# Attention scores in three 64-row products, two heads at a time, in place of two 128-row products, one head at a time

## The chip, the cores and the metric

The kernel runs on one core of a Trainium2 chip. The metric is the device time of one execution in microseconds. Before the change it was 1157.51 us, the median of 3 runs (1156.15 to 1157.67). The engines that matter are TensorE (matmul; its weight loads are shown apart), VectorE, ScalarE and GpSimd; in the profile's names PE and PEld, DVE, ACT and POOL. SyncE issues the DMAs.

## The reference

Two layers of a trunk with two token mixers side by side. There are 512 latent tokens and 256 context tokens of 1024 channels; all heads have 64 channels.

```python
def _attend(q, k, v):
    s = jnp.einsum('bqkgd,btkd->bkgqt', q, k).astype(jnp.float32) * (HEAD_DIM ** -0.5)
    p = jax.nn.softmax(s, axis=-1).astype(v.dtype)
    return jnp.einsum('bkgqt,btkd->bqkgd', p, v)
...
    a_att = _na_latent(qa, ka, va, cka, cva, rpb, rows)     # 8 heads, 8x16 window + all context keys
    b_att = _gqa_latent(qb, k_all, v_all)                   # 8 query heads on 2 key heads, all 768 keys
    out_x = _merge(a_att, b_att, a_z, b_z, g_a, g_b, w_o_a, w_o_b, w_out)
    x_new = x + gate_x * out_x
    if update_ctx:                                          # layer 0 only
        c_a_att = _attend(cqa, cka, cva).reshape(B, L, NA_WIDTH)
        c_b_att = _attend(cqb, ckb, cvb).reshape(B, L, GQA_WIDTH)
```

`_na_latent` is the neighbourhood attention: a latent query sees a window of latent keys with a learned bias, and all 256 context keys without one. `_gqa_latent` is the grouped attention. In layer 0 the context tokens attend to the context keys too, in both.

## The kernel before

Everything that is multiplied is kept as two parts of the fast 32-bit matmul type: `hi`, the rounded value, and `lo`, the rest. A product is then `hi*hi + hi*lo + lo*hi`, three matmuls (`mm3`, L339 to L343). Projections run over 128 channels at a time; activations lie with channels on partitions, so a matmul has a 128x128 stationary part (whose load is the PEld row) and up to 512 columns that stream.

A head has only 64 channels. Two heads lie in one group of 128 partitions, the even head in the lower 64 and the odd head in the upper 64. The scores of a head use all 128 rows of the array in this way: `stage_q` (L694, casts at L699, L700) makes a tile `qs` with q's hi part in the head's own half and q's lo part in the other half. `stage_k` (L685) makes `kh`, which has k's hi part in both halves (L688, L689), and `kl`, which has k's lo part in the own half (L690) and zeros, or in the grouped attention the same lo part (L692), in the other. Two matmuls then make the scores (`scores`, L703, and L783 for the tiles with two runs of keys): `qs` against `kh` gives hi*hi + lo*hi, `qs` against `kl` gives hi*lo.

The neighbourhood attention (`na_first`, `na_scores`) handles a head as 4 tiles of 128 queries with 512 keys each, of which 256 are window and 256 context. The bias is added, and the row's maximum found, in one VectorE operation from PSUM (L786), then comes exp (L789) and the normalization (`softmax_tail`, L639; its multiplication on VectorE at L644, or on GpSimd at L647). The grouped attention (`gq_first`, `gq_scores`) has 4 tiles of 128 queries with 768 keys, so 1.5 PSUM banks each: the maximum at L943, exp from PSUM at L945. In layer 0 every head also has one context tile (`ctx_scores`): two blocks of 128 queries by 256 keys.

`na_values` and `gq_values` then transpose the probabilities on the array (L655, L657), split them in hi and lo (`transpose_split`, ScalarE at L660, VectorE at L661) and multiply them with the values (L809 to L820, L960, L961). `head_out` (L664) multiplies the result into the gate.

`pipeline` (L825) sets the order for a whole attention: the scores of head h, then the values of head h-1, then a share of `fill`, which is a list of projection matmuls that need nothing of the attention. The text of the program gives priorities; a planner places each instruction on its engine's queue from a model of time, so an instruction with a later place in the text can go ahead of one that has to wait. `behind` (L376) ties instructions of one engine to the order in which they were written. `bg` is a list of background steps on VectorE, dot products of the modulation weights (`ada_steps`, L220, each tile of weights loaded by a DMA).

The PSUM has 8 banks. Of these the neighbourhood attention gives scores three tiles of one bank (`s`) and values one (`v`), and the grouped attention gives scores two tiles of two banks and values one. A tile of probabilities, `p`, comes from a pool with `NP_NA` and `NP_GQ` buffers for layers 0 and 1.

## Time and profile before

| what | value |
|---|---|
| median of 3 runs | 1157.51 us |
| the profiled execution | 1154.84 us, span 1153.1 us |
| granted TensorE clock | 0.998 |
| PE busy | 1123.5 us (97%) |
| DVE busy | 811.9 us (70%) |
| ACT busy | 573.2 us (50%) |
| POOL busy | 494.5 us (43%) |

The span is the time from the first to the last instruction of the profiled execution; a little of its time lies around the span. By the start times of the matmuls of the scores (L706, L707, L783) the neighbourhood attention of layer 0 lies at about 152 to 320 us of the span, the grouped attention of layer 0 at 386 to 600, the neighbourhood attention of layer 1 at 780 to 893, and the grouped attention of layer 1 at 948 to 1086. A row of the timeline gives the start, the duration, the engine, the line, the operation with its output and inputs, and the shape; the duration of a matmul runs from its start to the modelled end of its pass through the array, so that matmuls that follow each other overlap in the rows. What a matmul takes from the array's time is the distance between the starts.

### The profile page before, as it was taken

To read this page: it belongs to the slowest core of one execution; us is meant where nothing else is said; L and a number is where in the kernel's file an instruction comes from. 1 tells how busy PE (TensorE), PEld (TensorE's weight loads), DVE (VectorE), ACT (ScalarE), POOL (GpSimd) and SP (SyncE) were. 2 spreads that over 40 slices of the span, in tenths; PEclk is the share of its full clock that TensorE was granted. 3 is DMA by queue.
4 is the path that set the end of the run, shared out by engine and by line. 5 is a ranking of instruction groups with operands and counts; after the bars stand their busy time and mean duration, and the time that the engine had idled before them with its cause. 6 is when DMAs were issued, how large, how long until landed. Compare 5 with 4: busy or idle time off the path is not lost.

```text
span 1153.1 us, 17284 instructions
## 1 busy us (share of the span) xinstructions
PE 1123.5 (97%) x6078; PEld 949.3 (82%) x6078; DVE 811.9 (70%) x1508; ACT 573.2 (50%) x1167; POOL 494.5 (43%) x459
## 2 busy tenths in 40 slices
PE   5999999999999999999999999999999999999998
PEld 4688888889988888878788887888888988887786
DVE  4566688897474687688587755569787765898563
ACT  5453266666433465566330265446666445766521
POOL 3372354454266243354411126245553664365311
PEclk9999999999999999999999999999999999999999
DMA  9544222233342332470353523543332333142133
GB/s 370 194 125 137 69 85 65 73 115 96 115 130 60 109 102 73 65 279 19 114 179 101 174 74 110 173 108 114 107 105 84 110 101 101 65 173 92 62 130 93
DMA packets 87999, 134.04 MB, mean 116 GB/s; under 512 B 10628, under 2 KB 52584, under 8 KB 86248
## 3 DMA queue, kind: packets, MB, share of 16 engines
q1 hardware_dynamic: 87912, 132.94, 36.7%
q8 instruction: 48, 0.79, 0.3%
q14 instruction: 39, 0.32, 0.1%
HBM read 115.58 MB, written 17.32 MB: 115 GB/s over the span
## 4 chain that ended last, share of the span: by engine, by line
PE 83%; DVE 7%; issue 3%; POOL 2%; ACT 2%; DMA 1%; ACTq 0%; POOLq 0%; DVEq 0%
PE psx L341 12%; PE psx L343 12%; PE psx L342 12%; PE psf L341 9%; PE psf L342 9%; PE psf L343 9%; PE pst L657 4%; PE pss L706 2%; PE pss L707 2%; PE psv L961 2%; PE pss L783 1%; PE psv L960 1%; PE pst L417 1%; DVE wlo L328 1%; DVE ptl L661 1%
## 5 line engine op out<-in xcount | busy, mean ns | idle before, releaser
L661 DVE TENSOR_TENSOR ptl<-pst,pth 128x512 fp32r<-128x512 f32 (+1 forms) x176 | 116.0, 672 | 46.4 <-ACT pth L660 45.4
L660 ACT CAST pth<-pst 128x512 fp32r<-128x512 f32 (+1 forms) x176 | 99.2, 576 | 87.6 <-PE pst L657 56.3
L328 POOL TENSOR_TENSOR wlo<-raw,whi 128x512 fp32r<-128x512 f32 x68 | 95.5, 1408 | 107.2 <-ACT whi L326 86.2
L341 PE MATMUL psf<-hx,whi 128*128 128x512 f32 (+1 forms) x368 | 139.2, 378 | 0.0
L342 PE MATMUL psf<-hx,whi 128*128 128x512 f32 (+1 forms) x368 | 138.1, 375 | 0.0
L343 PE MATMUL psf<-hx,wlo 128*128 128x512 f32 (+1 forms) x368 | 137.8, 374 | 0.0
L341 PE MATMUL psx<-whi,hx 128*128 128x512 f32 (+1 forms) x368 | 137.6, 375 | 0.0
L342 PE MATMUL psx<-wlo,hx 128*128 128x512 f32 (+1 forms) x368 | 135.8, 369 | 0.0
L343 PE MATMUL psx<-whi,hx 128*128 128x512 f32 (+1 forms) x368 | 133.4, 369 | 0.0
L314 POOL TENSOR_TENSOR wlo<-raw,whi 128x512 fp32r<-128x512 f32 x44 | 61.4, 1397 | 140.4 <-ACT whi L311 123.8
L326 ACT CAST whi<-raw 128x512 fp32r<-128x512 f32 x136 | 82.4, 621 | 55.6 <-DMA raw<-in_w_in_dram 39.6
L311 ACT CAST whi<-raw 128x512 fp32r<-128x512 f32 x96 | 58.7, 623 | 102.1 <-PE psx L343 38.6
L657 PE MATMUL pst<-ident,p 128*128 128x128 f32 x640 | 99.9, 272 | 1.4 <-DVE ptl L661 0.9
L328 DVE TENSOR_TENSOR wlo<-raw,whi 128x512 fp32r<-128x512 f32 x68 | 72.1, 1062 | 28.4 <-ACT whi L326 27.8
L657 PEld LDWEIGHTS pst<-ident,p 128*128 128x128 f32 x640 | 77.8, 140 | 13.3 <-DVE ptl L661 1.6
L646 POOL TENSOR_SCALAR r<-r 128x1 f32<-128x1 f32 x64 | 23.1, 361 | 151.8 <-DVE r L641 144.2
L647 POOL TENSOR_TENSOR p<-p,r 128x512 f32<-128x512 f32 (+1 forms) x64 | 83.4, 1304 | 5.0
L341 PEld LDWEIGHTS psx<-whi,hx 128*128 128x128 f32 x368 | 69.7, 189 | 11.7 <-issue 0.8
L343 PEld LDWEIGHTS psx<-whi,hx 128*128 128x128 f32 x368 | 69.4, 189 | 11.8
L343 PEld LDWEIGHTS psf<-hx,wlo 128*128 128x128 f32 x368 | 69.4, 188 | 11.8
L342 PEld LDWEIGHTS psx<-wlo,hx 128*128 128x128 f32 x368 | 69.7, 189 | 10.8
L341 PEld LDWEIGHTS psf<-hx,whi 128*128 128x128 f32 x368 | 69.4, 189 | 10.8 <-ACT zt L502 0.2
(239 smaller groups left out, 3032.6 us busy)
## 6 DMA issues: line engine op xcount, KB each, us to landing
raw<-in_w_in_dram SPq DMA_DIRECT2D x168, 256.0 KB, 2.9
rawb<-in_w_ada_dram SPq DMA_DIRECT2D x64, 256.0 KB, 2.8
gs<-zt SPq DMA_DIRECT2D x32, 256.0 KB, 2.0
raw<-in_w_out_dram SPq DMA_DIRECT2D x32, 256.0 KB, 2.9
tg<-gs SPq DMA_DIRECT2D x4, 1536.0 KB, 7.5
rawx<-in_w_ada_dram SPq DMA_DIRECT2D x4, 1024.0 KB, 6.4
rawy<-in_w_ada_dram SPq DMA_DIRECT2D x4, 1024.0 KB, 12.2
raw<-in_w_o_a_dram SPq DMA_DIRECT2D x16, 256.0 KB, 2.8
```

The lines of the kernel that those rows point to most:

```text
L311: S.copy(hi[:, :n], raw[:, :n])
L314: e.tensor_tensor(lo[:, :n], raw[:, :n], F(hi[:, :n]), ALU.subtract)
L326: S.copy(hi, raw)
L328: lo_eng(i).tensor_tensor(lo, raw, F(hi), ALU.subtract)
L341: T.matmul(ps, lhs[0], rhs[0], start=first, stop=False)
L342: T.matmul(ps, lhs[0], rhs[1], start=False, stop=False)
L343: T.matmul(ps, lhs[1], rhs[0], start=False, stop=last)
L646: G.tensor_scalar(r[:, i:i + 1], r[:, i:i + 1], 0.5, None, ALU.mult)
L647: G.tensor_tensor(p[:, c0:c1], p[:, c0:c1], r[:, i:i + 1].to_broadcast([128, c1 - c0]), ALU.mult)
L657: T.transpose(pt[:, c0:c0 + 128], src, ident)
L660: S.copy(hi[:, n0:n1], pt[:, n0:n1])
L661: V.tensor_tensor(lo[:, n0:n1], pt[:, n0:n1], F(hi[:, n0:n1]), ALU.subtract)
```

## The change

The scores are no longer made from stacked halves. For a pair of heads `stage_pair` makes one hi tile and one lo tile of 128 partitions for q, and for the neighbourhood attention one of each for k; in the lower 64 partitions lies the even head, in the upper 64 the odd one. (In the grouped attention both heads of a pair have the same key head, and `stage_k` puts its hi and its lo part in both halves.) `products` lists for each run of columns three matmuls over the 64 rows of one head: hi*hi, hi*lo, lo*hi. `abreast` issues the lists of an even and an odd head in turns, and ties all of them to that order on TensorE.

`attend` replaces `pipeline`. It goes in steps. At step s the even head of a pair handles its tile s (modulo the number of tiles of a head, 5 in layer 0 with the context tile and 4 in layer 1), and the odd head lies two steps behind. At the two first and the two last steps of an attention there is one head alone. There are 22 steps for an attention in layer 0 and 18 in layer 1. The scores of a step lie in one PSUM tile, one half for each head: 1024 columns (2 banks) in the neighbourhood attention and 2048 (4 banks) in the grouped one, and there is one buffer of it. The values of a head are written once the next head's probabilities are complete.

The bias has buffers for the even and for the odd head; for the odd head the two blocks of 256 keys are read and written in the other order (`key_first`). The background steps `gate_steps((0,))` of layer 0 move from the neighbourhood attention to the projections of the values and queries ahead of it. The buffers of `p` change.

```diff
-NP_NA = (7, 8)
+NP_NA = (8, 9)
-NP_GQ = (10, 11)
+NP_GQ = (8, 11)
+NS_GQ = 2
...
-            bg = ada_steps(1, range(16), (0,), 2, hp["p"])
+            bg = ada_steps(1, range(16), (0,), 2, hp["p"]) + gate_steps((0,), hp["p"])
...
-        per_bg = -(-len(bg) // (2 + qt))
+        per_bg = -(-len(bg) // (5 + qt if first else 2 + qt))
...
-            if t > 2:
+            if t > (0 if first else 2):
                 run(bg, per_bg)
...
+            def stage_pair(src, n, tag, eng):
+                hi = att["p"].tile([128, n], F32R, tag=tag + "h", name=nm(tag + "h"), bufs=att["ns"])
+                lo = att["p"].tile([128, n], F32R, tag=tag + "l", name=nm(tag + "l"), bufs=att["ns"])
+                S.copy(hi, src[:, :n])
+                eng.tensor_tensor(lo, src[:, :n], F(hi), ALU.subtract)
+                return hi, lo
...
-            def scores(ps, q, kh, kl, cuts):
-                for c0, n, sl in cuts:
-                    T.matmul(ps[:, c0:c0 + n], q, sl(kh), start=True, stop=False)
-                    T.matmul(ps[:, c0:c0 + n], q, sl(kl), start=False, stop=True)
+            def products(ps, q, k, e, i, cuts):
+                res = []
+                for c0, n, sl in cuts:
+                    for m, (a, b) in enumerate(((0, 0), (0, 1), (1, 0))):
+                        o, r = ps[:, c0:c0 + n], sl(rows(k[b], e))
+                        if len(r.shape) > 2:
+                            o = o.rearrange("p (s n) -> p s n", s=r.shape[1])
+                        res.append((n, lambda o=o, r=r, a=a, m=m: T.matmul(
+                            o, rows(q[a], e)[:, 128 * i:128 * i + 128], r, start=m == 0, stop=m == 2)))
+                return res
+            def abreast(lists):
+                put, had = (lambda fn: fn()), [0] * len(lists)
+                while any(lists):
+                    i = min((i for i in range(len(lists)) if lists[i]), key=lambda i: had[i])
+                    n, fn = lists[i].pop(0)
+                    had[i] += n
+                    put(fn)
+                    put = lambda fn: behind(ON_PE, fn)
...
-            open_ps(x=1, s=(3, 512), v=(1, 512))
+            open_ps(x=1, s=(1, 1024), v=(2, 512))
...
+            def attend(fill, spread, n, stage, products_of, probs_of, values_of, last=None, bg=[]):
+                per, lag, nf = (5 if first else 4), 2, len(fill)
+                staged, probs, ready = {}, {h: [] for h in range(8)}, []
+                def values():
+                    h = ready.pop(0)
+                    values_of(h, probs.pop(h))
+                for s in range(4 * per + lag):
+                    att["bg"] = bg if s > 2 * per or pm["n"] == 1 else []
+                    todo = [divmod(s - lag * e, per) + (e,) for e in range(2) if 0 <= s - lag * e < 4 * per]
+                    w = 512 if n <= 512 else 1024
+                    bank = psw(2 * w, "s")
+                    lists = []
+                    for j, i, e in todo:
+                        if i == e == 0:
+                            staged[j] = stage(j)
+                        ps = bank[:, w * e:w * e + (n if i < 4 else 512)]
+                        lists.append(ctx_products(ps, *staged[j], e) if i == 4 else
+                                     products_of(2 * j + e, i, *staged[j], ps))
+                    abreast(lists)
+                    for j, i, e in todo:
+                        h = 2 * j + e
+                        ps = bank[:, w * e:w * e + (n if i < 4 else 512)]
+                        probs[h].append(ctx_probs(ps) if i == 4 else probs_of(h, i, ps))
+                        run(att["bg"], 1)
+                        if i == per - 1:
+                            ready.append(h)
+                            if len(ready) == 2:
+                                values()
+                            run(fill, len(fill) - (nf - nf * min(h + 1, spread) // spread))
...
-            open_ps(s=(2, 1024), v=(1, 512))
+            open_ps(s=(1, 2048), v=(1, 512))
```

More of the change, by code (lines that the diff above doesn't have):

```diff
@@ L674, in rows, with stage_k @@
                 return a[64 * half:64 * half + 64]
[L676 to L685 removed]
+            def stage_k(src, e, kh, kl):
                 k = rows(src, e)
@@ L690, in stage_k @@
                 G.tensor_tensor(rows(kl, e), k, F(rows(kh, e)), ALU.subtract)
-                if dup:
-                    S.copy(rows(kl, 1 - e), F(rows(kl, e)))
-            def stage_q(src, e):
-                n = 768 if first else 512
-                qs = att["p"].tile([128, n], F32R, tag=f"qs{e}", name=nm("qs"), bufs=1)
-                q = rows(src, e)[:, :n]
-                S.copy(rows(qs, e), q)
-                V.tensor_tensor(rows(qs, 1 - e), q, F(rows(qs, e)), ALU.subtract)
-                return qs
@@ L709, in cut, with ctx_products @@
+            def abreast(lists):
[6 more added lines that the diff above has]
+                    put = lambda fn: behind(ON_PE, fn)
             def cut(a, b):
                 return lambda k: k[:, a:b]
-            def ctx_scores(q, kh, kl):
-                pss = ps_score()
-                for i in range(2):
-                    scores(pss, q[:, 512 + 128 * i:640 + 128 * i], kh, kl,
-                           [(256 * i, 256, cut(512, 768))])
+            def ctx_products(ps, q, k, e):
+                return [p for i in range(2) for p in products(ps[:, 256 * i:256 * i + 256], q, k, e, 4 + i,
+                                                              [(0, 256, cut(512, 768))])]
@@ L718, in ctx_scores, with ctx_probs @@
+            def ctx_probs(pss):
                 mx = sp.tile([128, 2], F32, tag="mx", name=nm("mx"), bufs=8)
@@ L760, in load_bias @@
+            na_es = open_att(f"na{l}", 512, NP_NA[l], NT_NA, 2)
+            bias = att["p"].tile([128, 5, 256], F32, tag="bias", name=nm("bias"), bufs=1)
+            V.memset(bias[:, 2], 0.0)
+            for b in (1, 4):
+                V.memset(bias[0:64, b, 128:256], NEG)
+                V.memset(bias[64:128, b, 0:128], NEG)
             def load_bias(h):
-                nc.sync.dma_start(bint[:, 0:256], bias_int[l, h])
+                b = 3 * (h % 2)
+                nc.sync.dma_start(bias[:, b], bias_int[l, h])
```

151 lines of the change are left out of this document (53 added, 98 removed).

## The prediction

> **What bounds the kernel now.** I read the page's busy shares and its chain first, then the table of windows over the attentions, and last the timeline, for what one matmul takes. From the page:
>
> ```profile
> span 1153.1 us, 17284 instructions
> ...
> PE 1123.5 (97%) x6078; PEld 949.3 (82%) x6078; DVE 811.9 (70%) x1508; ACT 573.2 (50%) x1167; POOL 494.5 (43%) x459
> ...
> PE 83%; DVE 7%; issue 3%; POOL 2%; ACT 2%; DMA 1%; ACTq 0%; POOLq 0%; DVEq 0%
> ```
>
> The chain that ended last is TensorE for 83%. That could hide slack in single stages, so the next view splits it: the projections ahead of the first attention, then the neighbourhood attention (NA) of layer 0, the grouped one (GQ) of layer 0, NA and GQ of layer 1. Columns: window, length, busy time of each engine.
>
> ```profile
> 54.00:152.00 98.00, 98.00 (x473) 81.67 (x472) 63.87 (x129) 37.38 (x63) 42.50 (x36) 1.00 0.40 117
> 152.00:320.00 168.00, 167.65 (x1073) 150.68 (x1073) 133.40 (x282) 98.52 (x223) 77.80 (x73) 1.00 0.30 89
> 386.00:600.00 214.00, 208.83 (x1258) 182.00 (x1257) 165.59 (x300) 118.19 (x243) 82.89 (x71) 1.00 0.36 115
> 780.00:893.00 113.00, 111.33 (x598) 93.73 (x597) 96.65 (x185) 72.98 (x152) 58.63 (x57) 1.00 0.33 102
> 948.00:1086.00 138.00, 134.93 (x701) 110.26 (x700) 106.01 (x162) 86.17 (x165) 64.22 (x59) 1.00 0.30 101
> ```
>
> TensorE is full in each of them: in the four attentions together 622.74 of 633 us. So a microsecond of array time saved or spent in an attention counts nearly whole, and work taken off the other engines counts nothing. The granted clock is 1.00 throughout. What a matmul takes of the array is the distance of starts, read here in GQ:
>
> ```profile
> 385.95 0.40 PE L706 MATMUL pss<-gk,qs 128*128 128x512 f32 x1
> 386.18 0.39 PE L707 MATMUL pss<-gk,qs 128*128 128x512 f32 x1
> 386.42 0.28 PE L706 MATMUL pss<-gk,qs 128*128 128x256 f32 x1
> 386.53 0.28 PE L707 MATMUL pss<-gk,qs 128*128 128x256 f32 x1
> 386.65 0.39 PE L706 MATMUL pss<-gk,qs 128*128 128x512 f32 x1
> ```
>
> 512 columns take 0.23 us (385.95 to 386.18) and 256 take 0.12 (386.53 to 386.65). The weight load lies beside the stream before it.
>
> **What the scores take now.** These are the matmuls against the hi keys; each has a twin against the lo keys (L707, L783):
>
> ```profile
> L706 PE MATMUL pss<-gk,qs x144: 276/283/504, 385.9 to 1061.1; 128*128 128x256 f32 x80, 128*128 128x512 f32 x64
> L943 DVE TENSOR_REDUCE mx<-pss x64: 937/948/958, 386.9 to 1061.6; 128x1 f32<-128x768 f32 x64
> L945 ACT ACTIVATE p<-pss,mx x64: 888/903/926, 387.8 to 1066.6; 128x768 f32<-128x768 f32 x64
> L945 ACT ACTIVATION_READ_ACCUMULATOR p<-pss,mx x64: 188/193/221, 388.6 to 1067.4; 128x1 f32 x64
> L706 PE MATMUL pss<-kh,qs x48: 220/282/392, 152.5 to 871.5; 128*128 128x128 f32 x16, 128*128 128x384 f32 x16, 128*128 128x256 f32 x16
> L783 PE MATMUL pss<-kh,qs x48: 387/394/497, 152.6 to 880.8; 128*128 128x512 f32 x48
> ```
>
> In runs of 512 columns (128 + 384 make one) there are 64 in GQ and 16 + 48 = 64 in NA; of 256 there are 80 + 16 = 96. Twice each: 2 x (128 x 0.23 + 96 x 0.12) = 81.9 us.
>
> **The products, if the halves run side by side.** Two heads then need three passes where they needed four, but the first two and last two steps of each attention have one head, which needs three passes where it needed two. By steps, each as long as its longer list: an NA step is 3 x 0.23 = 0.69 us with one head or two (the context tile, 6 x 0.12, fits), a GQ step 3 x (0.23 + 0.12) = 1.05. NA: (22 + 18) x 0.69 = 27.6. GQ: (22 + 18) x 1.05 = 42.0, less 0.3 for the one step of layer 0 that is a lone context tile. Sum 69.3, so **-12.6 us**. A plain three quarters would have been -20.5; the lone steps and the shorter context lists take 8 of it.
>
> No row of the trace shows two 64-row matmuls side by side. The nearest is L190, where four products lie beside each other in groups of 32 columns of the array. The same rows show what it costs to get in and out of a divided array, which I take as the main term:
>
> ```profile
> 29.91 0.40 PE L343 MATMUL psx<-whi,hx 128*128 128x512 f32 x1
> 30.24 1.06 PE L190 MATMUL pst<-rawx,scol 128*32 128x512 f32 x8
> ...
> 31.12 1.04 PE L190 MATMUL pst<-rawy,scol 128*32 128x512 f32 x8
> 32.10 0.50 PE L341 MATMUL psx<-whi,hx 128*128 128x512 f32 x1
> 32.43 0.39 PE L342 MATMUL psx<-wlo,hx 128*128 128x512 f32 x1
> ```
>
> ```profile
> 30.70 0.13 PEld L190 LDWEIGHTS pst<-rawy,scol 128*32 128x32 f32 x4 [0.30 <-issue]
> 31.13 0.13 PEld L190 LDWEIGHTS pst<-rawy,scol 128*32 128x32 f32 x4 [0.30 <-issue]
> ```
>
> Groups of four start every 0.43 us (30.70, 31.13: each load goes in as the group ahead begins), so four do run together: eight in a row would have ended far later than 1.06 us otherwise. Backwards, the first group streamed from 30.27, forwards the fourth ended at 31.13 + 2 x 0.43 = 31.99. **Entry**: the last whole-array matmul streamed until 29.91 + 0.23 = 30.14, so 0.13 us were lost. **Exit**: L342 began at 32.43, so L341 streamed from 32.20, 0.21 after the fourth group's end; its own row is 0.50 long in place of 0.40, the rest being the wait for its weights. In both places the weights are loaded only when the stream ahead has ended. For entry that load was small:
>
> ```profile
> L190 PEld LDWEIGHTS pst<-rawx,scol x32: 106/108/110, 12.6 to 47.0; 128*32 128x32 f32 x32
> L706 PEld LDWEIGHTS pss<-gk,qs x144: 186/188/194, 385.7 to 1060.9; 128*128 128x128 f32 x144
> ```
>
> The change's loads have 128 columns, 0.08 us more, so 0.21 for entry too: **0.42 us per round trip**. One row speaks of a change in rows instead of columns, at the start of the span:
>
> ```profile
> 3.70 0.18 PEld L149 LDWEIGHTS pst<-ident,csl 16*128 16x128 f32 x1 [3.70 <-DVE csl L143]
> 3.92 0.18 PEld L153 LDWEIGHTS pst<-ident,stg 68*128 68x128 f32 x1
> ```
>
> ```profile
> 393.98 0.49 PE L657 MATMUL pst<-ident,p 128*128 128x128 f32 x3
> ```
>
> From a 16-row to a 68-row transpose the loads are 0.22 apart, with no wait named, where transposes of one height follow each other at (0.49 - 0.27) / 2 = 0.11. Rows seem to cost something too, though this is one pair of instructions. The Trainium skill (TensorEngine Tiling (Array Packing), Key Properties) says that changing the tiling mode drains the array, while another tile of the same mode does not; that agrees with the 0.13 and 0.21 us here, and no run here shows it yet for halves of rows.
>
> How many round trips? One score tile with one buffer means that a step cannot follow the last one until VectorE or ScalarE have read it, at least 2 x 0.95 us in GQ, and TensorE fills that time with whole-array work (it is full). So each of the 2 x (22 + 18) = 80 steps is a trip of its own: 80 x 0.42 = **+33.6 us**. Bounds: 0 if rows need no drain, and above, some trips more where a transpose of higher priority splits a step's list; I take 80. Break-even is 12.6 / 80 = 0.16 us a trip, under the 0.34 that the rows show even with the small load.
>
> **The rest.**
>
> ```profile
> L688 DVE CAST kh<-ka x16: 544/558/1649, 147.7 to 858.4; 64x768 fp32r<-64x768 f32 x16
> L690 POOL TENSOR_TENSOR kl<-ka,kh x16: 1829/1847/2546, 148.4 to 859.1; 64x768 fp32r<-64x768 f32 x16
> L700 DVE TENSOR_TENSOR qs<-qa,qs x16: 952/1772/2578, 148.9 to 859.7; 64x768 fp32r<-64x768 f32 x8, 64x512 fp32r<-64x512 f32 x8
> L220 DVE CUSTOM_DVE_ANT_0 rawb<-rawb,cb x64: 675/691/1780, 91.2 to 765.4; 128x512 f32<-128x512 f32 x64
> L220 DVE DVE_READ_ACCUMULATOR2_ANT asum<- x112: 74/82/85, 91.1 to 766.1; 128x1 f32 x112
> ```
>
> Staging by pairs: VectorE loses 16 casts of 0.56 (L688) and half of the 32 subtractions of 0.95 or more (GQ's included), over 24 us; ScalarE and GpSimd lose about half of theirs. 0 us, because TensorE is full; it only widens the others' slack. The subtraction of k on GpSimd (1.85 us) now stands ahead of a pair's second product. Two buffers let it run a pair ahead; uncovered it is 1.85 us once at each NA's start, so 0 to 4 us, taken as 0. The 16 dot products that move (0.69 + 0.08 each, 12.3 us) raise VectorE in the projections from 63.87 to about 76 of 98 us; their eight weight loads and one of vectors go onto SyncE's queue there, ahead of later projection weights, and wait in it for a free buffer. TensorE has not idled in that window; without that cover a late weight tile costs 1 to 3 us. Taken as 0. The odd head's swapped bias blocks and the doubled bias buffer: same count and size, 0.
>
> The single score tile: in GQ a step is 1.05 + 0.42 on TensorE, two reductions of 0.95, the second exp of 0.90 and its 0.19: 4.5 us before the next can begin. 18 steps are 81 of the 138 us of layer 1, so other work covers it; taken as 0 here, a rival below.
>
> **Sum** against the profiled execution: 1154.84 - 12.6 + 33.6 = 1175.8. That execution lies 2.7 us under the median of 1157.51, so the prediction is **1178 us**, 1.8% slower. Its own range, trips at 0.34 to 0.5 us: 1172 to 1186.
>
> **Rivals.** *No drain between whole array and halves* (the other side). Place: each step. The side-by-side rows are columns, and the one row pair that speaks for rows is thin; against it, those 0.11 us extra. It decides below 0.16 us a trip. At 0 the time is 1157.5 - 12.6 = 1145; with some stalls of the single tile up to 1154.
>
> *The halves do not run side by side.* Then six passes stand where four stood: +81.9 / 2 = +41, 1198 without the trips and 1232 with them. Against it: four column groups do overlap at L190. The Trainium skill (TensorE: Matmul & The Clock Gate, Measured speedup vs the span model) has 3.07 for four row tiles in place of 4, so something between; by that ratio, as an estimate from that page, a pair's pass would be a third longer and the prediction some 17 to 20 us higher.
>
> *The single score tile becomes the bound in GQ.* Each reduction and exp can queue behind a split's parts:
>
> ```profile
> L661 DVE TENSOR_TENSOR ptl<-pst,pth 128x512 fp32r<-128x512 f32 (+1 forms) x176 | 116.0, 672 | 46.4 <-ACT pth L660 45.4
> ```
>
> At 4.5 + 4 x 0.67 = 7.2 us a step, 18 steps are 129 us and the last heads' values come on top: it decides from about 7 us a step. In layer 0 eight `p` buffers for the ten tiles of a pair make steps wait for `gq_values` as well. On top of the trips 5 to 15 us, 1183 to 1193.
>
> *A trip near 0.16 us*: no change.
>
> **Numbers.** Trips as measured 0.47, with the single tile as bound 0.12, halves in series 0.09: slower 0.68. No drain 0.26: faster. Near break-even 0.06: within 0.2%, about what a measurement here can tell from no change. Outside 1146 to 1199 I leave the lower tenth (no drain and no stall) and the serial case. So the range is 1146 to 1199.
>
> **What would show it.** Right: in the timeline of an attention, pairs of score matmuls that start within some 0.02 us, with pairs 0.23 apart, a hole of about 0.2 us in weight loads and streams on both sides of each step, TensorE still full, attentions longer by about 5 us each. Wrong: scores whose weights load beside the stream ahead (no drain); starts 0.23 apart one by one (series); TensorE idle with VectorE or ScalarE as releaser (the single tile).

## The result and the profile after

The changed kernel takes 1209.95 us (median of 4 runs, 1209.16 to 1215.65) against 1157.08 us of the kernel before on the same chip (4 runs, 1156.15 to 1157.67). The ratio is 1.0468, with a 95% interval from 1.0435 to 1.0501. It is slower, as forecast, but by 52.9 us where 20.5 were forecast, and the time lies above the range that was given (1146 to 1199).

From the page of the profiled execution after:

```profile
span 1207.6 us, 17643 instructions
...
PE 1157.1 (96%) x6318; PEld 944.0 (78%) x6318; DVE 767.6 (64%) x1474; ACT 554.2 (46%) x1143; POOL 467.5 (39%) x451
...
PE 84%; DVE 6%; issue 3%; ACT 2%; POOL 2%; DMA 1%; ACTq 0%; POOLq 0%; DVEq 0%
```

The span grew by 54.5 us. The chain is still TensorE, and VectorE, ScalarE and GpSimd each have less to do. The table of windows shows the stages in the prediction's order: the projections ahead of the first attention, NA and GQ of layer 0, NA and GQ of layer 1. Columns: window, length, then the busy time of TensorE, its weight loads, VectorE, ScalarE and GpSimd, the granted clock, the DMA share and GB/s.

```profile
54.00:152.60 98.60, 98.59 (x474) 81.76 (x472) 73.81 (x158) 37.06 (x63) 43.12 (x36) 1.00 0.46 135
152.60:320.40 167.80, 167.68 (x1074) 143.59 (x1074) 101.09 (x231) 89.22 (x208) 56.81 (x61) 1.00 0.25 77
...
393.80:602.10 208.30, 189.03 (x1159) 154.47 (x1159) 144.39 (x248) 101.85 (x216) 74.53 (x66) 0.98 0.29 97
814.70:939.40 124.70, 120.35 (x640) 92.20 (x640) 75.89 (x175) 66.95 (x143) 48.25 (x52) 1.00 0.29 89
994.80:1139.00 144.20, 138.45 (x755) 106.52 (x755) 98.48 (x157) 83.67 (x160) 63.25 (x58) 1.00 0.28 94
```

The windows that were given for the kernel before, 152 to 320 and 386 to 600 above all, reach past the ends of the attentions of layer 0. By their last value matmul these end at 311.7 and 567.6 us, and those of layer 1 lie at 781.1 to 893.3 and 948.6 to 1084.5. GQ of layer 0 before is therefore this row, and not the one of 214 us:

```profile
385.90:567.60 181.70, 177.72 (x1079) 154.64 (x1079) 140.93 (x252) 106.28 (x220) 75.15 (x65) 1.00 0.32 96
```

So this attention grew by 26.6 us. One stage stands out after the change. In GQ of layer 0 TensorE is without work for 19.3 of 208.3 us, and its clock is at 0.98. In the other three attentions it is busy for 167.68 of 167.80, 120.35 of 124.70 and 138.45 of 144.20 us, so those are long because TensorE has more to do.

Busy time cannot tell a useful pass from a drained array, so the rest of this document uses one accounting for all kernels. What a matmul takes of the array is the distance between its modelled end and that of the matmul before. In unbroken runs this is 0.228 us for 512 columns, 0.119 for 256 and 0.109 for a transpose; anything beyond it is a wait (half-rate streams after a wait are counted in it). A run of 64-row matmuls is taken as one trip: its passes are counted from its first end to its last, and what is lost on its two sides beyond the waits that the trace names is the trip's cost. Each attention goes from its first score matmul to its last value matmul. The columns "before" and "after" add up to the span less 9.3 and 9.4 us, nearly all of which lies ahead of the first matmul and after the last.

| us | before | after | difference | forecast |
|---|---|---|---|---|
| everything that is not scores | 1016.6 | 1016.6 | 0.0 | 0 |
| passes of the scores | 81.4 | 72.7 | -8.7 | -12.6 |
| trips into the halves and back | none | 37.3 (95 trips) | +37.3 | +33.6 (80 trips) |
| TensorE's waits | 45.8 | 71.6 | +25.8 | 0 |
| of these, GQ of layer 0 | 8.1 | 29.7 | +21.6 | 0 |

The three differences make 54.4 us, which is the growth of the span. What the forecast said of a trip can be read from one step. These are TensorE's rows around a step of NA in layer 1, where a row stands for several matmuls if it ends in x2:

```profile
881.33 0.40 PE L817 MATMUL psv<-pth,va 128*128 128x512 f32 x1
881.57 0.39 PE L344 MATMUL psf<-hx,wlo 128*128 128x512 f32 x1
881.89 0.50 PE L701 MATMUL pss<-kh,qh 64*128 64x512 f32 x2
882.23 0.40 PE L701 MATMUL pss<-kl,qh 64*128 64x512 f32 x2
882.46 0.39 PE L701 MATMUL pss<-kh,ql 64*128 64x512 f32 x2
882.78 0.50 PE L818 MATMUL psv<-ptl,va 128*128 128x512 f32 x1
883.12 0.40 PE L817 MATMUL psv<-pth,va 128*128 128x512 f32 x1
```

and the weight loads of the same stretch:

```profile
881.33 0.19 PEld L344 LDWEIGHTS psf<-hx,wlo 128*128 128x128 f32 x1
881.89 0.19 PEld L701 LDWEIGHTS pss<-kh,qh 64*128 64x128 f32 x2 [0.36 <-PE psf L343]
881.99 0.19 PEld L701 LDWEIGHTS pss<-kl,qh 64*128 64x128 f32 x2
...
882.78 0.19 PEld L818 LDWEIGHTS psv<-ptl,va 128*128 128x128 f32 x1 [0.36 <-issue]
```

Two matmuls of 64 rows stand in each row, 0.40 us long, where one of 128 rows has 0.40 too, and the second and third pair start 0.23 apart: the halves do run side by side, with no loss. The load for L344 went in at 881.33, while the matmul ahead of it streamed. The load for the first pair waited until 881.89, after L344's stream had ended at 881.57 + 0.23 = 881.80. The first pair then streamed from 882.23 - 0.23 = 882.00, so entry cost 0.20 us. The last pair's stream ended at 882.46 + 0.23 = 882.69, L818 was loaded at 882.78 and streamed from 883.12 - 0.23 = 882.89: exit cost 0.20 as well. The Trainium skill (TensorEngine Tiling (Array Packing), Key Properties) says that a change of the tiling mode drains the array, without a price; for halves of rows the price here is 0.40 us a trip.

### The profile page after: what moved, and what is told of

It is laid out like the page before. It is cut to its first block, busy times and chain, and to the rows that moved or that the text cites. A ratio compares the mean times of both kernels' runs of the same rounds, so it can differ in the third digit from the quotient of the medians.

```text
span 1207.6 us, 17643 instructions
## 1 busy us (share of the span) xinstructions
PE 1157.1 (96%) x6318; PEld 944.0 (78%) x6318; DVE 767.6 (64%) x1474; ACT 554.2 (46%) x1143; POOL 467.5 (39%) x451
## 4 chain that ended last, share of the span: by engine, by line
PE 84%; DVE 6%; issue 3%; ACT 2%; POOL 2%; DMA 1%; ACTq 0%; POOLq 0%; DVEq 0%
PE psx L342 12%; PE psx L344 12%; PE psx L343 12%; PE psf L342 10%; PE psf L343 9%; PE psf L344 9%; PE pss L701 7%; PE pst L658 5%; PE psv L977 2%; PE psv L976 2%; PE pst L418 1%; DVE ptl L662 1%; DVE wlo L329 1%; DMA rawb<-in_w_ada_dram 1%; ACT pth L661 1%
## 5 line engine op out<-in xcount | busy, mean ns | idle before, releaser
L344 PE MATMUL psf<-hx,wlo 128*128 128x512 f32 (+1 forms) x368 | 137.6, 374 | 0.0
L344 PE MATMUL psx<-whi,hx 128*128 128x512 f32 (+1 forms) x368 | 133.7, 369 | 0.0
L658 PE MATMUL pst<-ident,p 128*128 128x128 f32 x640 | 100.9, 276 | 8.2 <-DVE ptl L662 8.0
L329 DVE TENSOR_TENSOR wlo<-raw,whi 128x512 fp32r<-128x512 f32 x68 | 75.0, 1102 | 42.3 <-ACT whi L327 42.1
L658 PEld LDWEIGHTS pst<-ident,p 128*128 128x128 f32 x640 | 77.8, 141 | 24.8 <-DVE ptl L662 9.7
L961 DVE TENSOR_REDUCE mx<-pss 128x1 f32<-128x768 f32 x64 | 60.6, 946 | 35.3 <-PE pss L701 35.2
L344 PEld LDWEIGHTS psf<-hx,wlo 128*128 128x128 f32 x368 | 69.4, 188 | 12.4 <-issue 0.4
L344 PEld LDWEIGHTS psx<-whi,hx 128*128 128x128 f32 x368 | 69.6, 189 | 11.8
```

The lines of the kernel that those rows point to most:

```text
L329: lo_eng(i).tensor_tensor(lo, raw, F(hi), ALU.subtract)
L344: T.matmul(ps, lhs[1], rhs[0], start=False, stop=last)
L658: T.transpose(pt[:, c0:c0 + 128], src, ident)
L961: V.tensor_reduce(mx[:, 0:1], ps, AX, ALU.max, negate=True)
```

## The experiments

All times of this section are medians of one batch each, given as the ratio to the kernel before in the same batch; the accounting is of the profiled execution.

### No halves at all

This asks whether the trips are what the change pays for. Every product runs over all 128 rows, in the changed kernel's order. The kernel so adds the channels of both heads of a pair into each score (in the grouped attention, with a key head that is the same in both halves), and has six passes a step in place of three.

```diff
-                        o, r = ps[:, c0:c0 + n], sl(rows(k[b], e))
+                        o, r = ps[:, c0:c0 + n], sl(k[b])
...
-                            o, rows(q[a], e)[:, 128 * i:128 * i + 128], r, start=m == 0, stop=m == 2)))
+                            o, q[a][:, 128 * i:128 * i + 128], r, start=m == 0, stop=m == 2)))
```

> Edit: each of the three products runs over all 128 rows, so it adds the channels of both heads of the pair (the scores are those of two heads summed; for the grouped attention q of both heads against the shared key head). There is no divided array and no second matmul beside the first. Theory 'trips': after the change the score matmuls took about 113 us of the array, 73 us of passes and 95 entries and exits at 0.42 us. With whole-array matmuls the entries and exits vanish (-40 us) and the passes stand one after the other (+50 us): 1215 to 1225 us, and no holes in the weight loads around the steps. Rival 'the holes are not the mode's, the time went to waits on the softmax': the passes add 50 us and nothing goes away: 1250 to 1265 us.

Measured: 1227.98 us, ratio 1.061 (1.0588 to 1.0631), 3 us above what the trips let expect. Passes take 122.1 us, 49.4 more than after; there are no trips, 37.3 less; the waits are 76.7. So the trips are real, and against six whole passes the halves save more than their trips cost: taking the division away costs 49.4 - 37.3 = 12.1 us net, and the waits put 5.1 us on top. The waits in GQ of layer 0 are still 30.0 us, so the divided array does not make them.

### One list after the other

This asks what the turns are for. `abreast` issues the whole list of the even head and then that of the odd one.

```diff
-                    i = min((i for i in range(len(lists)) if lists[i]), key=lambda i: had[i])
+                    i = next(i for i in range(len(lists)) if lists[i])
```

> Edit: the lists of the two heads are issued one after the other instead of in turns; nothing else. Theory 'pairs run side by side only if they are neighbours in the queue': the paired steps take six passes in place of three, some 45 to 50 us more, 1250 to 1262 us, less what now covers the waits. Rival 'the array overlaps halves in whatever order they come': no change, 1207 to 1213 us.

Measured: 1232.89 us, ratio 1.0661 (1.0643 to 1.0678), between the two expectations. Passes rose by 19.5 us to 92.2; trips (38.4 us) and waits (73.2) stayed. The trace of a GQ step shows why it is between:

```profile
468.06 0.39 PE L344 MATMUL psf<-hx,wlo 128*128 128x512 f32 x1
468.38 0.72 PE L701 MATMUL pss<-gk,qh 64*128 64x512 f32 x2
468.94 0.40 PE L701 MATMUL pss<-gk,ql 64*128 64x512 f32 x1
468.95 0.73 PE L701 MATMUL pss<-gk,qh 64*128 64x512 f32 x4
469.41 0.50 PE L701 MATMUL pss<-gk,ql 64*128 64x256 f32 x2
...
470.19 0.51 PE L976 MATMUL psv<-pth,vb 128*128 128x512 f32 x1
```

The first head's first two matmuls of 512 columns run alone from 468.38 on. The second head's list starts at 468.95, beside the first's third matmul (468.94), and from there on the two overlap until the first's list is done. The step takes 470.19 - 468.38 = 1.81 us. In the changed kernel the same twelve matmuls stand between 464.90 and 466.14, 1.24 us (rows further down). So a half need not wait until the other's list is done, but it starts late: by the order of the lists its first matmul is the seventh, and it ran beside the third. How far ahead the array reaches in general, this step does not show.

### One kind of attention alone

These two split the change. In the first the grouped attention is new, and NA and the place of the gate's dot products are as before. In the second NA and the moved dot products are new, and the grouped attention is as before. The edit puts the old functions beside the new ones; the lines that choose are these.

```diff
-            attend(fill, 9, 512, na_stage, na_products, na_probs, values_of(za, na_values))
+            pipeline(fill, 9, na_first, values_of(za, na_values), bg=bg)
```

> Edit: the grouped attention as after the change, the neighbourhood attention and the place of the gate dot products as before. Theory 'each attention pays for itself': the two grouped attentions were 27 and 8 us longer after the change, so 1157 + 35 = 1188 to 1196 us, the 20 us of extra waits in the one of layer 0 among them. Rival 'those waits come from what the neighbourhood attention leaves late': 1168 to 1178 us.

```diff
-            open_ps(s=(1, 2048), v=(1, 512))
+            open_ps(s=(2, 1024), v=(1, 512))
...
-            attend(fill, 8, 768, gq_stage, gq_products, gq_probs, values_of(zb, gq_values), early, bg)
+            pipeline(fill, 8, gq_first, values_old(zb, gq_values), early, bg)
```

> Edit: the neighbourhood attention (and the moved gate dot products) as after the change, the grouped attention as before with its 10 tiles of probabilities. Theory 'each attention pays for itself': +9 and +12 us, 1174 to 1182 us, with about 50 entries and exits at 0.42 us and passes 2 us shorter than before. Rival: as above, 1190 us or more.

Measured: GQ alone 1192.45 us, ratio 1.0315 (1.0297 to 1.0333); NA alone 1178.25 us, ratio 1.0194 (1.0179 to 1.0209). Together that is 0.0509 over 1, against the change's 0.0468: the two halves nearly add up. With GQ alone new, its layer-0 stage takes 208.1 us with 29.5 us of waits, as in the full change. With NA alone new, that stage takes 181.3 us with 7.8 us of waits, as before; the loss is then 19.9 us of trips against 2.3 us of passes saved. So NA loses by its trips, and GQ by trips and, in layer 0, by waits.

### More room for probabilities, and the gate's other half moved away

Theories for the waits in GQ of layer 0 were its eight buffers of `p`, and VectorE's load there. The first kernel also moves the second half of the gate's dot products out of that stage to the projections; the second gives `p` 11 buffers on top.

```diff
-            bg = ada_steps(1, range(16), (0,), 2, hp["p"]) + gate_steps((0,), hp["p"])
+            bg = ada_steps(1, range(16), (0,), 2, hp["p"]) + gate_steps((0, 1), hp["p"])
...
-            bg = gate_steps((1,), att["p"]) if first else []
+            bg = []
```

> Edit: the second half of layer 0's gate dot products moves too, from the grouped attention to the projections ahead of the neighbourhood attention; buffers unchanged (8 tiles of probabilities). It is the base for the next run, and tells whether VectorE's background work in the grouped attention makes the stalls. Theory 'buffers' and theory 'single score tile' both: little change, 1200 to 1212 us. Theory 'VectorE is too busy there': 5 to 12 us less.

```diff
-NP_GQ = (8, 11)
+NP_GQ = (11, 11)
```

> Edit: as the run before, and with the space freed 11 tiles of probabilities in place of 8 in the grouped attention of layer 0. Theory 'eight tiles for the ten of a pair hold the steps up': the 20 us of extra TensorE stalls of that attention shrink by 8 to 18 us against the run before. Rival 'the single score tile sets the pace': within 3 us of the run before.

Measured: 1221.76 us, ratio 1.0563 (1.0547 to 1.0579), and 1223.12 us, ratio 1.0578 (1.0558 to 1.0598). Waits in GQ of layer 0 are 22.6 us with 8 buffers and 23.7 with 11, and the times are 1.4 us apart, within the 3 us that were expected if the buffers do not matter. They bind little in this pair, though: in that stage ScalarE's exps wait 0.7 us for a buffer of `p` with 8 buffers here, where they wait 3.4 us in the changed kernel. The first kernel met neither expectation. With less VectorE work in the stage its waits are 7 us lower, but more was lost ahead, as the first attention begins at 166.2 in place of 152.6 us. TensorE's waits at the end of the projections, with 8 buffers:

```profile
PE pst L418 <- DVE y L406: 7.4, 4, 3.9
PE psf L342 <- DVE za L505: 2.3, 1, 2.3
```

The prediction had costed the move of 16 dot products at nothing; the change's own 16 indeed cost nothing (152.6 against 152.5 us), and 16 more cost 13.6.

### No lag

Without the lag both heads of a pair stand at the same tile, and no step has one head alone (20 and 16 steps).

```diff
-                per, lag, nf = (5 if first else 4), 2, len(fill)
+                per, lag, nf = (5 if first else 4), 0, len(fill)
```

> Edit: the odd head no longer lies two steps behind, so there are 20 and 16 steps in place of 22 and 18 and no step with one head alone. Theory 'trips and lone steps': 8 steps less, 8 us of passes and 3 to 4 us of entries and exits, 1195 to 1202 us. Rival 'the waits on the single score tile set the pace and the values of two heads now come at once': the gain is eaten, 1205 to 1220 us.

Measured: 1213.39 us, ratio 1.0498 (1.047 to 1.0526). Passes fell by 8.0 us to 64.7 and trips by 4.4 to 32.9 (82 of them), and the waits rose by 13.5 to 85.1. That is the rival's range: what the lone steps cost in passes the forecast had right, and the lag pays for itself in waits.

### The held VectorE operation

In GQ of layer 0 the longest single wait of the changed kernel stands behind an operation of VectorE that lasted 8.93 us. The rows of VectorE, of GpSimd, and of TensorE, after:

```profile
501.36 8.93 DVE L329 TENSOR_TENSOR wlo<-raw,whi 128x512 fp32r<-128x512 f32 x1 [2.93 <-ACT whi L327]
```

```profile
499.95 5.40 POOL L545 TENSOR_TENSOR gal<-za,gah 128x768 fp32r<-128x768 f32 x3
505.31 1.46 POOL L648 TENSOR_TENSOR p<-p,r 128x768 f32<-128x768 f32 x1
506.73 1.79 POOL L545 TENSOR_TENSOR gal<-za,gah 128x768 fp32r<-128x768 f32 x1
508.49 1.25 POOL L329 TENSOR_TENSOR wlo<-raw,whi 128x512 fp32r<-128x512 f32 x1
```

```profile
511.68 1.11 PE L658 MATMUL pst<-ident,p 128*128 128x128 f32 x4 [6.15 <-DVE ptl L662]
...
513.02 0.63 PE L977 MATMUL psv<-ptl,vb 128*128 128x512 f32 x1
513.44 0.63 PE L976 MATMUL psv<-pth,vb 128*128 128x512 f32 x1
```

VectorE's operation ended at 510.29, 0.55 us after the last of an unbroken run of GpSimd operations (508.49 + 1.25 = 509.74), which had begun at 497.26. The kernel for this puts GpSimd's subtractions of L545 onto VectorE.

```diff
-                G.tensor_tensor(R(dst[1][:, f, :ntok]), sv[:, f, :ntok], dst[0][:, f, :ntok], ALU.subtract)
+                V.tensor_tensor(R(dst[1][:, f, :ntok]), sv[:, f, :ntok], dst[0][:, f, :ntok], ALU.subtract)
```

> Edit: the subtractions of the split of the gated values (L545) on VectorE instead of GpSimd; the rest as after the change. In the grouped attention of layer 0 one VectorE operation lasted 8.9 us while GpSimd ran six operations without a break, four of them of this line; TensorE stood still for 6.1 us of it and then ran at half rate for a microsecond. Theory 'VectorE was held until GpSimd had a gap': no VectorE operation over 3 us is left, 6 to 10 us less, 1199 to 1205 us. Rival 'it was only the place where a wait shows': the wait comes elsewhere, 1207 to 1214 us.

Measured: 1211.35 us, ratio 1.0493 (1.0458 to 1.0529). No VectorE operation in that stage is held any longer, and its waits are still 28.2 us; they only lie elsewhere. TensorE's largest waits there:

```profile
PE psf L342 <- ACT zt L503: 4.7, 5, 2.4
PE psf L342 <- DVE tg L579: 3.4, 3, 1.6
PE pst L658 <- DVE ptl L662: 2.1, 2, 1.6
```

So the held operation is one place where the stage's waits show, and not their cause.

### One score tile in the old order, and two in the new

This pair asks about the single score tile directly. The first kernel is the kernel before, with one score tile in the grouped attentions in place of two.

```diff
-            open_ps(s=(2, 1024), v=(1, 512))
+            open_ps(s=(1, 1024), v=(1, 512))
```

> The kernel before, with one two-bank score tile in the grouped attentions where it had two; nothing else is changed. If it is the single buffering of the scores that makes TensorE wait in the grouped attention (most of all in layer 0, where the change has 29.7 us of waits against 8.1), the old order must show it too: the next scores can only start after the exp of the tile before, so the waits in the grouped attention of layer 0 rise from 8 to 18 or more, and the time to 1167 to 1190. If it is the order of the change (two heads at once, values of a head only after the next head's probabilities, projections handed out per head), single buffering alone costs little: waits within 4 us of the kernel before, time 1155 to 1162.

The second is the changed kernel with a tile for each head, in the same banks.

```diff
-            open_ps(x=1, s=(1, 1024), v=(2, 512))
+            open_ps(x=1, s=(2, 512), v=(2, 512))
...
-                    bank = psw(2 * w, "s")
+                    banks = {e: psw(w, "s") for j, i, e in todo}
...
-                        ps = bank[:, w * e:w * e + (n if i < 4 else 512)]
+                        ps = banks[e][:, :n if i < 4 else 512]
...
-            open_ps(s=(1, 2048), v=(1, 512))
+            open_ps(s=(2, 1024), v=(1, 512))
```

> The changed kernel, with one score tile for each head in place of one tile for both, in the same banks; a head's half comes free by itself, and steps of one head have two buffers. If the waits come from the two heads' scores being held together until the later one is read, the grouped attention of layer 0 loses 8 us or more of its 29.7 us of waits, time 1198 to 1203. If a step has to wait for both halves anyway, since its lists go in turns, nothing moves: 1207 to 1212, waits 26 to 32.

Measured: one tile in the old order 1221.45 us, ratio 1.0563 (1.0546 to 1.0581); two in the new 1219.36 us, ratio 1.0549 (1.0533 to 1.0565). The first went the way that the theory of the tile said, and nearly twice as far as its upper end of +34 us: the time rose by 65.7 us. The second met neither expectation in time. Its waits fell as the theory said, and the time rose all the same. The accounting:

| us | before | before, one tile | after | after, two tiles |
|---|---|---|---|---|
| passes | 81.4 | 81.4 | 72.7 | 82.1 |
| trips (number) | none | none | 37.3 (95) | 59.3 (151) |
| waits | 45.8 | 109.2 | 71.6 | 48.8 |
| waits in GQ, layer 0 | 8.1 | 39.3 | 29.7 | 14.8 |
| waits in GQ, layer 1 | 8.4 | 40.3 | 11.1 | 7.7 |

One score tile makes TensorE wait in the old order too: 63.4 us, half in each GQ. The scores then wait for the exp that reads the tile before them; in GQ of layer 0 this is among TensorE's largest waits:

```profile
PE pss L706 <- ACT p L945: 5.9, 5, 2.3
```

A part of the 63.4 us is the clock: its mean in GQ of layer 0 is 0.94, where it is 1.00 before, so TensorE also ran slower after its waits. Two tiles in the new order bring the waits down to 48.8 us, 3.0 over the kernel before. But the halves then come free at different times, and a step falls apart into several runs: 56 more trips (+22.0 us), and matmuls that no longer find their partner (+9.4 us of passes). The single tile buys whole steps and pays in waits; two tiles do the reverse and, by the accounting, end 8.6 us worse. In GQ of layer 0 the waits fall by 14.9 us but the stage gets only 7.0 us shorter (201.3 us for 208.3), since trips and passes come in their place. Two tiles that hold both heads would take twice 4 banks in the grouped attention and leave none for the values, so no run has them.

How the tile is held is seen in a GQ step of the changed kernel, here the one whose scores run from 449.64 to 450.95 us. VectorE's reductions of its two halves:

```profile
452.25 0.94 DVE L961 TENSOR_REDUCE mx<-pss 128x1 f32<-128x768 f32 x1
...
454.33 0.94 DVE L961 TENSOR_REDUCE mx<-pss 128x1 f32<-128x768 f32 x1
```

ScalarE's exps of the two halves, and what stands between them:

```profile
453.23 0.90 ACT L963 ACTIVATE p<-pss,mx 128x768 f32<-128x768 f32 x1 [1.96 <-DVE mx L961]
...
454.29 1.07 ACT L661 CAST pth<-pst 128x512 fp32r<-128x512 f32 x2
456.22 0.38 ACT L503 ACTIVATE zt<-psf 128x256 f32<-128x256 f32 x1 [0.86 <-PE psf L344]
458.34 0.59 ACT L661 CAST pth<-pst 128x512 fp32r<-128x512 f32 x1 [1.73 <-PE pst L658]
461.68 0.90 ACT L963 ACTIVATE p<-pss,mx 128x768 f32<-128x768 f32 x1 [2.76 <-PE pst L658]
```

and TensorE's next step:

```profile
464.90 0.73 PE L701 MATMUL pss<-gk,qh 64*128 64x512 f32 x4
465.46 0.40 PE L701 MATMUL pss<-gk,ql 64*128 64x512 f32 x2
465.70 0.40 PE L701 MATMUL pss<-gk,qh 64*128 64x256 f32 x4
465.93 0.28 PE L701 MATMUL pss<-gk,ql 64*128 64x256 f32 x2
466.14 0.50 PE L976 MATMUL psv<-pth,vb 128*128 128x512 f32 x1
```

The second half was reduced by 455.27, and its exp came at 461.68. ScalarE first did casts of the values, the last of which waited for transposes. From 458.93 on it stood idle for 2.76 us until further transposes (L658) ran. By the program the exp and these transposes share only the tiles `p`: the exp needs a free buffer, and the transposes are the last to read one. So this step was so long in part for want of a `p` buffer; over the whole stage such waits come to 3.4 us in two places. The next scores started 2.3 us after that exp had ended, 15.3 us after the last step's. This is a long step: the 22 steps of the stage start on average 9.1 us apart (393.8 to 584.1 in 21 distances). In this one TensorE found other work nearly all the time. That this work is then missing later is likely but not shown.

### Handing out the other work differently

Two kernels change only when the projections that fill the grouped attentions are handed out: in equal shares after every step, or with three elevenths held back to the end.

```diff
-                            run(fill, len(fill) - (nf - nf * min(h + 1, spread) // spread))
+                            if n == 512:
+                                run(fill, len(fill) - (nf - nf * min(h + 1, spread) // spread))
+                    if n == 768:
+                        run(fill, len(fill) - (nf - nf * (s + 1) // (4 * per + lag)))
```

> The changed kernel, with the projections that fill the grouped attentions handed out in equal shares after every step (22 and 18) in place of an eighth after each head. If the waits come from the bunches in which that work is handed out (two heads end two steps apart, and then three steps pass without any), the grouped attention of layer 0 loses 8 us or more of its 29.7 us of waits, time 1196 to 1203. If they come from the distance between steps that reductions, exps and buffers set, the planner has the same work at hand in either case and the waits stay at 25 to 33, time 1206 to 1214.

```diff
-            attend(fill, 8, 768, gq_stage, gq_products, gq_probs, values_of(zb, gq_values), early, bg)
+            attend(fill, 11, 768, gq_stage, gq_products, gq_probs, values_of(zb, gq_values), early, bg)
```

> The changed kernel, with three elevenths of the projections that fill the grouped attentions held back until the last step, in place of all of them handed out with the last head. In the last 30 us of the grouped attention of layer 0 the changed kernel keeps TensorE busy for 25.4 us at a clock of 0.94, against 29.2 at 1.00 before. If that end lacks only cover that was used up too early, its loss of about 8 us falls to 3 or less with no new waits ahead of it: time 1201 to 1206. If the waits of the steps have to be covered by the same projections, what the end wins comes back as waits between the steps: 1207 to 1214, with the waits of the whole stage at 26 to 33 us.

Measured: 1212.32 us, ratio 1.0485 (1.0468 to 1.0503), and 1214.77 us, ratio 1.0503 (1.0485 to 1.052). Waits in GQ of layer 0 are 30.4 and 29.9 us. The order of the other work moves nothing. In the first of the two no VectorE operation is held in that stage, and it waits all the same, which clears the held operation once more.

What two tiles did not take away is the end of the stage. The last 30 us of GQ in layer 0, in windows, before:

```profile
537.60:567.60 30.00, 29.21 (x180) 24.99 (x180) 20.35 (x35) 16.53 (x32) 14.36 (x11) 1.00 0.08 27
```

after:

```profile
572.00:602.10 30.10, 25.40 (x138) 19.71 (x137) 20.49 (x34) 16.15 (x34) 11.56 (x9) 0.94 0.27 96
```

and with two tiles:

```profile
572.00:604.00 32.00, 26.37 (x139) 19.71 (x139) 20.61 (x33) 15.80 (x34) 13.74 (x11) 0.95 0.27 90
```

TensorE does 180 matmuls there before and 138 or 139 after, at a lower clock. By the accounting the last 28 us after hold 8.4 us of the stage's waits, and the last 21 us with two tiles 9.9, where the last 32 us before hold 1.8. Outside the end the waits are 6.3 us before, 21.3 after and 4.9 with two tiles. So the waits in the body of the stage go with the single tile. Why TensorE has so little to do at its end in both, whether for the late last values or for projections used up before, is open: holding projections back did not mend it.

## Why the prediction was right or wrong

**Right: the mechanism and its price.** The forecast said that halves run side by side with pairs 0.23 us apart, that entry and exit drain the array for about 0.21 each with no load ahead, and that this outweighs the passes saved. The rows show pairs 0.23 apart and 0.20 on each side; by the accounting a trip is 37.3 / 95 = 0.39 us against 0.42. The price came from column groups, and held for halves of rows. How well the halves overlap could not be read there: the four column groups took 0.43 us together, a pair of halves takes 0.23. The rivals without a drain and with halves in series both fall: the first by the trip rows, the second by the kernel without turns and the one without halves, whose passes are 92.2 and 122.1 us against 72.7. With pairs 0.23 apart nothing is left of a pass that is a third longer either.

**Mis-sized: the number of trips and the passes.** There are 95 trips, not 80: 51 in the NAs where 40 steps were counted, and 44 in the GQs. The forecast named "some trips more where a transpose of higher priority splits a step's list" as a bound and took 80. The splits came, but mostly from other matmuls: of the 15 further runs twelve are split off by matmuls of the values (in one of them with transposes), eight of these in NA of layer 1, as at 856.86, 857.73 and 858.84 us; three are split off by projections at the start of an NA. The passes of the NAs are 30.8 us where 27.6 were worked out, while in GQ 41.8 us stand against 42.0 minus 0.3. The two terms, trips and passes, are 3.7 and 3.9 us too low.

**Wrong: the step "so other work covers it; taken as 0 here" on the single score tile.** It was a sum of the durations that a step needs at least (4.5 us), set against the stage's length, and for layer 1 alone. There it nearly held: the waits of that GQ rose by 2.7 us. It failed in layer 0, for which nothing had been worked out. The trace shows steps 9.1 us apart in GQ of layer 0, where each reduction and exp queues on VectorE and ScalarE behind the parts of the values; the rival had said this and put 7.2 us a step. It had the right trigger and too small a price, 5 to 15 us; the waits rose by 25.8 us, 21.6 of them in GQ of layer 0. The pair of kernels on the tile shows the cause: one tile alone makes 63.4 us of waits in the old order, and two tiles take 22.8 us out of the new one. Of the 25.8 us, about 15 (the body of that stage, 21.3 against 6.3) go with the tile; that all 15 could be won back is not shown, since with two tiles trips and passes took half their place. Some 6.6 us at that stage's end stay open, and the last 4.2 lie in the other stages.

**Right where nothing was expected.** The 16 moved dot products cost nothing, the first attention begins at 152.6 us against 152.5. The eight `p` buffers, named as a part of the rival, cost nothing that 11 would give back in the pair that tested it, though one step of the changed kernel waited 2.76 us for one. That less load on the other engines brings nothing was not tested alone, and it holds only where TensorE is full: in GQ of layer 0 less work on VectorE went with 7 us less of waits.

**The range** had room for both causes together, but at too small a price: trips as measured and the tile as bound were given as 1183 to 1193 with a chance of 0.12. With 25.8 us for the tile in place of 5 to 15 the same sum is 1178 + 25.8 = 1203.8; the other 6 us are the two mis-sized terms (7.6), less 1.4 by rounding and by how the two profiled executions stand to their medians. (The range "1172 to 1186" for trips at 0.34 to 0.5 us ends at 1185 when it is added up; nothing rests on that.)

None of these kernels is faster than the one before. In each that divides the array a trip costs 0.39 to 0.40 us, where a full step saves 4 x 0.23 - 3 x 0.23 = 0.23 us in NA and 0.35 us (0.23 + 0.12) in GQ: by these numbers a step has to share its trip with another one, and so hold twice the PSUM, before the halves can pay; no run tests that.

## What to carry to other kernels

Dividing the array for short contractions pays only where the run of divided work between two whole-array stretches saves more than the drain on both sides, here 0.40 us; count the runs after the planner has split them, not the steps in the text. When a change turns double-buffered scores into single-buffered ones, price the whole cycle of the buffer with the queues that its readers stand in, and not the durations of the readers; that other work fills the gap has to be worked out for every stage, as it nearly held in layer 1 and failed in layer 0. The cheapest test of such a term is the old kernel with one buffer less.

## What was not expected of the hardware

**A VectorE operation was held for most of an unbroken run of GpSimd.** It took 8.93 us after (quoted above), with GpSimd at work from 497.26 to 509.74, where the same line took 1.80 us before, beside four GpSimd operations that ran unbroken for 8.00 us:

```profile
491.33 1.80 DVE L328 TENSOR_TENSOR wlo<-raw,whi 128x512 fp32r<-128x512 f32 x1 [3.69 <-ACT whi L326]
```

```profile
488.97 8.00 POOL L544 TENSOR_TENSOR gal<-za,gah 128x768 fp32r<-128x768 f32 x4
```

Without GpSimd's subtractions the hold was gone; but it was gone too in the kernel that hands out the projections in equal shares, which has them. The Trainium skill (GPSIMD Engine Reference, Specifications) says that GpSimd shares its memory interface with VectorE and that operations with two inputs in SBUF contend; this operation has two. Why one is held and another not stays open. In the old order with one score tile the same operation took 6.62 us and ended at 492.2, 1.1 us before GpSimd's run did.

**After the wait of 6.15 us TensorE ran at half rate.** Its matmuls of 512 columns at 513.02 and 513.44 start 0.42 apart in place of 0.23, and the granted clock of that stretch is 0.50:

```profile
511.60:514.50 2.90, 2.82 (x9) 2.44 (x10) 1.84 (x5) 1.66 (x4) 0.72 (x1) 0.50 0.68 213
```

The clock's mean is 0.75 from 505.0 to 511.6 us and 0.94 from 514.5 to 520.0. If it is either 1 or 0.5, the half rate lasted from about 508.3 to 515.1 us: it began within the wait and went on for 3.4 us after the work had come back at 511.68. The Trainium skill (TensorE: Matmul & The Clock Gate, The HAM clock gate) has this gate with a window of about 3.4 us: an idle window halves the clock and a busy one restores it. The trace agrees, with 6.8 us, which is two such windows. So a long wait costs more than its length, here some 1.7 us (half of 3.4; an estimate).

**Out of turns the halves overlap in part.** Six matmuls of each half took 1.81 us with one list after the other, 1.24 us in turns.
